# Gate and modulation sums of a hybrid diffusion layer: from per-row multiply-adds with a matmul at the end, to multiply-and-sum along the row with weights laid out by channel

## The chip, the cores and the metric

The kernel runs on one core of one Trainium2 chip. The metric is the device time of one execution in microseconds (us), as a median of runs. The core has a matmul engine (TensorE, PE, whose weight loads are listed as PEld), a vector engine (VectorE, DVE), a scalar engine (ScalarE, ACT), GpSimd (POOL) and SyncE (SP), which here only issues DMAs. ACT issues some DMAs as well.

## The reference

Two layers run over 256 latent tokens and 256 context tokens of width 2048, all in float32. Layer 0 mixes neighbourhood attention (16 heads of 128) with a bidirectional state-space scan (SSD); layer 1 is a gated short convolution. Each layer is modulated by a conditioning vector `c`:

```python
def adaln(cond, w, b):
    m = jax.nn.silu(cond) @ w + b
    return jnp.split(m, 3, axis=-1)          # shift, scale, gate
...
shift, scale, gate = adaln(c, ada_w[i], ada_b[i])
h = modulate(rms_norm(x, norm_g[i]), shift[:, None], scale[:, None])
...
x = x + gate[:, None] * y
```

`ada_w` is 2 x 2048 x 6144. Shift and scale of layer 0 are needed at once, and another part of the kernel makes them. This document is about the rest, which is needed later: the gate of layer 0 (2048 channels), then shift and scale of layer 1 (4096) and its gate (2048). That is one vector of 2048 numbers, silu(c), against 8192 columns of 2048 weights, 64 MB of loads.

## The kernel before, in words

Each float32 weight matrix is loaded in pieces of 128 x 1024 into one of five `raw` buffers (nine at the start), and split into a high part (ACT, L419) and a low part (DVE, L426), so that three fast matmuls make one exact product. PE streams through these pieces: layer 0's input projection for keys, values and queries in eight segments (`ada_gen`, L702, makes the modulated activations for each), then gates, SSD inputs and the remaining heads, then the output projection, layer 1's input projection and its output projection. Attention heads, SSD groups and norms run between, as generators.

Nothing sets the order at run time. While the program is built, a planner (`Plan`, L38) keeps an estimated clock for every engine and for DMA. Work stands in three lists, `urgent`, `side` and `back`; `pump` (L277) writes out a generator's next instructions once the planner thinks that their inputs are ready in time, and each engine then runs its own instructions in the order in which they were written. Names: `W_("DVE", tiles)` means that DVE is about to use these tiles, `when(f)` waits for a condition, `issue` (L364) takes the next load from `loads` (weights) or `later` (the gate and modulation weights) as soon as a buffer is free, `give_raw` returns a buffer, and `hold` keeps the `back` list still at the start and in the norm of layer 1.

The sums of this document are `gemv_gen` (L799), the only task in `back`. `later_loads` (L504) lists its 128 loads, each 256 rows by 512 columns of `ada_w`: the 2048 inputs lie along partitions, the channels along the row. Per load two instructions (L817) multiply one 128 x 512 half with a per-partition scalar (silu(c), in `csil`) and add it to an accumulator `acc`. After 16 loads, two accumulators of 512 channels hold 128 partial sums each. Sixteen matmuls with a matrix of ones (L825) add up the partitions, DVE copies the result (L827), and ACT's DMA (L830) writes it to `mrow` in DRAM. The bias enters as a row loaded into the accumulator (L808). Eight such rounds make 16 blocks of 512 channels. After block 11, shift and scale of layer 1 are read back from DRAM as 32 rows (L835), turned by one PE transpose (L838) and stored in `M1`, one channel per partition. `n_back` tells the readers how far the sums are: `res_gen` (L1587) reads the first gate, `turn_gen` (L1625) `M1`, `fin_gen` (L1957) the second gate.

Of the kernel before, what the change touches and what calls it, by code (L numbers as in the profile page):

```python
# [11 lines left out]
ALU = mybir.AluOpType  # L12
AX = mybir.AxisListType

D = 2048
KB = 16
# [122 lines left out]


@with_exitstack
def kernel(ctx: ExitStack, tc, x, cx, ada0, w0, ada_w, ada_b, w_in, w_out, sc_in, sc_out, rpb, small, const,
                       strict, rows, out):
    nc = tc.nc
    PS = bass.MemoryType.PSUM
# [4 lines left out]
    V, S, G, T, DMA = nc.vector, nc.scalar, nc.gpsimd, nc.tensor, nc.sync  # L150
    DMA2 = nc.scalar
    plan = Plan()
    E = plan.add

    def st(shape, tag, dt=F32, name=None):
        return sb.tile(list(shape), dt, tag=tag, name=name or tag, bufs=1)

    def drt(shape, name):
        return dr.tile(list(shape), F32, name="dram_" + name)


    NTMP, NHALF, NRAW, NW = 9, 8, 5, 3
# [27 lines left out]
    two = lambda ap: ap.rearrange("p (a b) -> p a b", a=2)  # L190
    four = lambda ap: ap.rearrange("p (a b) -> p a b", a=4)

    def mm(o, l, r, start, stop):
        E(T.matmul(o, l, r, start=start, stop=stop, skip_group_check=True))  # L194

    def turn(o, i):
        k = i.shape[0]
        E(T.transpose(o, i, ident if k == 128 else ident[:k, :k]))  # L198
# [136 lines left out]
    def bank():  # L335
        return take(free_b)

    def give(pool, *bs):
        pool.extend(bs)
# [17 lines left out]
    RAW, HL = {}, {}  # L357
# [6 lines left out]
    def issue():  # L364

        while (loads or later) and (free_r or (loads and callable(loads[0]))):
            if loads and callable(loads[0]):
                loads.popleft()()
                continue
            if later and (not loads or (ngem[0] < loads[0][7] and len(RAW) - ngem[0] >= 5 - loads[0][7])):  # L370
                kind, key, w, r0, nb, c0, n = later.popleft()
                ngem[0] += 1
            elif loads:
                kind, key, w, r0, nb, c0, n, _ = loads.popleft()
            else:
                return
            raw = raw_()
            v = raw[:, :nb * n].rearrange("p (b c) -> p b c", b=nb)
            if w is ada0 or w is w0:
# [124 lines left out]
    def later_loads():  # L504
        started[0] = True
        free_r[:] = [a for a in free_r if a.tensor.name not in spare_names]
        for n in range(16):
            lay = 0 if n < 4 else 1
            c0 = 4096 + n * 512 if n < 4 else (n - 4) * 512
            for k in range(8):  # L510
                later.append(("g", ("gem", n, k), ada_w[lay], k * 256, 2, c0, 512))

    CK, CV, CQ, CG = (lambda a: COL_K + a * 512), (lambda a: COL_V + a * 512), (lambda a: a * 512), (lambda a: COL_G + a * 512)

# [276 lines left out]
        got.add(("part", j, key, t))  # L791


    mrow = drt([4, D], "mrow")
    M1 = st([128, 2, KB], "M1")
    accs = st([128, 2, 512], "acc")
    n_back = [0]

    def gemv_gen():  # L799
        for n2 in range(0, 16, 2):  # L800

            yield W_("DVE", nb=0)
            E(V.memset(accs, 0.0))
            for n in (n2, n2 + 1):
                lay = 0 if n < 4 else 1
                c0 = 4096 + n * 512 if n < 4 else (n - 4) * 512
                acc = accs[:, n - n2, :]
                E(DMA.dma_start(acc[:1, :], ada_b[lay:lay + 1, c0:c0 + 512]))  # L808
                for k in range(8):
                    yield when(lambda: not (("gem", n, k) not in RAW))  # L810
                    yield W_("DVE", RAW["gem", n, k][1], acc)
                    raw, v = RAW.pop(("gem", n, k))
                    ngem[0] -= 1
                    for j in range(2):
                        if j:
                            yield W_("DVE", acc)
                        E(V.scalar_tensor_tensor(out=acc, in0=v[:, j], scalar=csil[:, 2 * k + j:2 * k + j + 1], in1=acc,  # L817
                                                 op0=ALU.mult, op1=ALU.add))
# [7 lines left out]
            yield W_("DVE", ps)  # L826
            E(V.tensor_copy(rowb, ps[:, :256]))  # L827
            give(free_b, ps)
            yield W_("AQ", rowb)
            E(DMA2.dma_start(mrow[n // 4, (n2 % 4) * 512:(n2 % 4) * 512 + 1024].rearrange("(m g c) -> g m c", m=2, g=4),  # L830
                             two(rowb[0:128:32, :])))
            n_back[0] = n
            if n == 11:
                yield W_("AQ", mrow[2:3, 1024:])
                E(DMA2.dma_start(mrb[:32, :], mrow[1:3, :].rearrange("r (b c) -> (r b) c", c=128)))  # L835
                yield W_("PE", mrb, nb=1)
                pm = bank()
                turn(pm[:, :32], mrb[:32, :])  # L838
                yield W_("DVE", pm)
                E(V.tensor_copy(M1.rearrange("p r b -> p (r b)"), pm[:, :32]))  # L840
                give(free_b, pm)
                n_back[0] = 11.5

    rowb = st([128, 256], "rowb")
    mrb = rowb[:, :128]

    spawn(back, gemv_gen())
    hold[0] = True
# [1108 lines left out]
    def fin_gen(n, ps):  # L1957
        cols = slice(n * 512, (n + 1) * 512)
        yield when(lambda: n_back[0] >= 15)
        gb, o = tmp(), tmp()  # L1960
        yield W_("SP", mrow[3:4])
        E(DMA.dma_start(gb, mrow[3, cols].partition_broadcast(128)))
# [32 lines left out]
    force(lambda: not urgent, (urgent,))  # L1995


_INS = ['x', 'cx', 'ada0', 'w0', 'ada_w', 'ada_b', 'w_in', 'w_out', 'sc_in', 'sc_out', 'rpb', 'small', 'const', 'strict', 'rows']


# [55 lines left out]
```

## Time and profile before

| | |
|---|---|
| Median of 3 runs | 1769.88 us (1769.78 to 1770.18) |
| Profiled execution | 1768.15 us |
| Its span (first to last instruction) | 1766.2 us |
| PE, DVE, ACT busy in the span | 99%, 71%, 44% |
| The old sums on DVE (L817) | 256 instructions, 191.6 us |
| Their loads | 128 of 512 KB, median 4.3 us from issue to landing |
| First and last sum begin | 166.8 us, 1491.3 us |

A line of instructions reads: line of the kernel, engine, operation, output tile <- input tiles, shapes and count; then busy time and the mean of one in ns, and after the bar the idle time of the engine just before them and what ended it. A timeline line reads: start, length (merged neighbours together), engine, line, operation, and in brackets idle time before it with what ended it. A line of waits reads: who <- whom, then us in total, times, longest. A line of stretches reads: from:to, length, then busy time and count of PE, PEld, DVE, ACT and POOL, then the granted PE clock (1.00 is full), DMA share and GB/s. A line of one source or tile reads: shortest, median and longest duration in ns, first and last start in us. Matmul durations overlap, since the engine is pipelined; the distance between starts tells the rate.

### The profile page before, as it was taken

What the parts mean: (1) busy time and instruction counts of PE and PEld (TensorE: products, weight loads), DVE (VectorE), ACT (ScalarE), POOL (GpSimd) and SP (SyncE); (2) the same over time, 40 slices, a digit from 0 to 9 for tenths busy, and PEclk for the clock granted to TensorE, in tenths of its full rate; (3) what the DMA queues carried; (4) which work ended last, traced back from release to release, by engine and by line L of the source; (5) the groups of instructions that cost most, each with busy time, mean ns of one, the idle gap of its engine ahead of it and who ended that gap; (6) DMA issues with size and microseconds to landing.
All of it is one profiled execution on the core that took longest, in us unless ns stands there. A gap on an engine that the chain in (4) does not pass through costs nothing.

```text
span 1766.2 us, 25384 instructions
## 1 busy us (share of the span) xinstructions
PE 1742.5 (99%) x9577; PEld 1464.8 (83%) x9577; DVE 1260.7 (71%) x1986; ACT 773.2 (44%) x1330; POOL 32.1 (2%) x28
## 2 busy tenths in 40 slices
PE   6999999999999999999999999999999999999998
PEld 4777988888888889888888898888888888888887
DVE  5657778878686878675878787787668776555554
ACT  5423544455242445342445344565445444444442
POOL 0000100001000001000001000000000000000000
PEclk9999999999999999999999999999999999999999
DMA  9977644666746666646666566667867877666563
GB/s 369 347 283 253 209 148 134 200 207 203 233 141 199 205 199 194 220 134 195 209 189 190 159 189 198 194 207 273 294 212 239 264 260 250 189 187 189 190 210 120
DMA packets 218138, 374.60 MB, mean 212 GB/s; under 512 B 32304, under 2 KB 69008, under 8 KB 218016
## 3 DMA queue, kind: packets, MB, share of 16 engines
q1 hardware_dynamic: 210704, 366.38, 64.1%
q10 hardware_dynamic: 7312, 6.61, 1.1%
q8 instruction: 75, 1.23, 0.3%
q14 instruction: 47, 0.39, 0.1%
HBM read 367.52 MB, written 6.72 MB: 212 GB/s over the span
## 4 chain that ended last, share of the span: by engine, by line
PE 90%; DMA 5%; DVE 4%; issue 1%; SPq 1%; ACT 1%; POOL 0%; DVEq 0%; ACTq 0%
PE bank L194 86%; PE bank L198 3%; DMA raw<-in_ada_w 2%; DVE acc L817 1%; DVE w L426 1%; DMA tmp<-dram_csr 1%; DMA raw<-in_w_in 1%; DMA raw<-in_ada 0%; DVE tmp L1241 0%; DMA raw<-in_sc_in 0%; DMA half<-in_rows 0%; SPq L1045 0%; DMA acc<-in_ada_b 0%; ACT w L419 0%; DVE tmp L981 0%
## 5 line engine op out<-in xcount | busy, mean ns | idle before, releaser
L419 ACT CAST w<-raw 128x1024 fp32r<-128x1024 f32 (+1 forms) x343 | 358.2, 1046 | 536.4 <-PE bank L194 458.9
L426 DVE TENSOR_TENSOR w<-raw,w 128x1024 fp32r<-128x1024 f32 (+1 forms) x343 | 414.8, 1213 | 179.7 <-ACT w L419 178.4
L194 PE MATMUL bank<-hH,w 128*128 128x256 f32 (+1 forms) x2064 | 489.2, 324 | 2.5 <-DVE w L426 2.5
L194 PE MATMUL bank<-w,hH 128*128 128x512 f32 x1280 | 405.8, 395 | 2.6 <-ACT hH L757 2.6
L194 PEld LDWEIGHTS bank<-hH,w 128*128 128x128 f32 x2064 | 345.0, 188 | 36.0 <-DVE w L426 3.5
L194 PE MATMUL bank<-hL,w 128*128 128x256 f32 (+1 forms) x1040 | 334.3, 322 | 0.0
L194 PEld LDWEIGHTS bank<-w,hH 128*128 128x128 f32 x1280 | 236.6, 188 | 54.6 <-issue 4.6
L194 PE MATMUL bank<-w,hL 128*128 128x512 f32 x640 | 249.3, 390 | 0.1
L817 DVE SCALAR_TENSOR_TENSOR acc<-raw,csil,acc 128x512 f32<-128x512 f32 x256 | 191.6, 748 | 74.7 <-DMA raw<-in_ada_w 64.2
L194 PEld LDWEIGHTS bank<-hL,w 128*128 128x128 f32 x1040 | 196.4, 189 | 14.9
L194 PE MATMUL bank<-w,h 128*128 128x512 f32 x768 | 180.1, 391 | 0.0
L194 PEld LDWEIGHTS bank<-w,h 128*128 128x128 f32 x768 | 143.4, 188 | 29.8 <-issue 0.4
L194 PEld LDWEIGHTS bank<-w,hL 128*128 128x128 f32 x640 | 120.1, 188 | 25.4 <-DVE hL L763 0.6
L194 PE MATMUL bank<-w,mix 128*128 128x512 f32 x588 | 138.8, 392 | 0.0
L194 PEld LDWEIGHTS bank<-w,mix 128*128 128x128 f32 x588 | 109.4, 188 | 22.6 <-issue 0.2
L1241 DVE SCALAR_TENSOR_TENSOR tmp<-bank,cwh,tmp 128x508 f32<-128x508 f32 (+1 forms) x96 | 71.1, 744 | 1.8
L194 PE MATMUL bank<-KL,h 128*128 128x512 f32 x264 | 63.9, 389 | 0.0
L194 PEld LDWEIGHTS bank<-KL,h 128*128 128x128 f32 x264 | 49.5, 188 | 10.2
L426 DVE TENSOR_TENSOR wL<-raw,wH 128x1024 fp32r<-128x1024 f32 x31 | 37.9, 1222 | 27.6 <-ACT wH L419 27.5
L194 PE MATMUL bank<-QT,h 128*128 128x512 f32 x168 | 55.9, 391 | 0.0
L194 PE MATMUL bank<-wH,h 128*128 128x512 f32 x168 | 55.6, 390 | 0.0
L426 DVE TENSOR_TENSOR QL<-raw,QT 128x1024 fp32r<-128x1024 f32 x32 | 39.1, 1222 | 23.1 <-ACT QT L419 22.6
(288 smaller groups left out, 1976.8 us busy)
## 6 DMA issues: line engine op xcount, KB each, us to landing
raw<-in_w_in SPq DMA_DIRECT2D x196, 512.0 KB, 4.1
raw<-in_ada_w SPq DMA_DIRECT2D x128, 512.0 KB, 4.3
raw<-in_sc_in SPq DMA_DIRECT2D x128, 512.0 KB, 4.6
raw<-in_w_out SPq DMA_DIRECT2D x64, 512.0 KB, 4.2
raw<-in_ada SPq DMA_DIRECT2D x36, 512.0 KB, 5.4
raw<-in_sc_out SPq DMA_DIRECT2D x32, 512.0 KB, 3.7
PT<-in_ada SPq DMA_DIRECT2D x16, 512.0 KB, 8.6
tmp<-dram_csr SPq DMA_DIRECT2D x32, 256.0 KB, 5.8
```

The costliest lines, as they stand in the source:

```text
L194: E(T.matmul(o, l, r, start=start, stop=stop, skip_group_check=True))
L198: E(T.transpose(o, i, ident if k == 128 else ident[:k, :k]))
L419: E(S.copy(H, v))
L426: E(V.tensor_tensor(out=Lo, in0=v, in1=H.bitcast(F32), op=ALU.subtract))
L817: E(V.scalar_tensor_tensor(out=acc, in0=v[:, j], scalar=csil[:, 2 * k + j:2 * k + j + 1], in1=acc, op0=ALU.mult, op1=ALU.add))
L1241: E(V.scalar_tensor_tensor(out=do, in0=di, scalar=cwh[:, 32 * k + ch:32 * k + ch + 1], in1=do, op0=ALU.mult, op1=ALU.add))
```

## The change

The weights for these sums are laid out anew before the launch: `adaT` holds, for each of the 64 blocks of 128 channels and each half of the 2048 inputs, a piece of 128 channels (partitions) by 1024 inputs (along the row). One instruction per load now multiplies a piece with silu(c) and sums along the row (`tensor_tensor_reduce`), into one column of `gp`. For that, silu(c) must lie along the row on every partition. It is turned once into a row by `rows_out` (a PE transpose, a DVE copy, a DMA of ACT to `crow` in DRAM), and half of it at a time is spread over all 128 partitions into `csb` by a DMA of SP. There are three stretches (16, 32 and 16 blocks: gate of layer 0, shift and scale of layer 1, gate of layer 1); in each, all blocks are summed over the first half of the inputs and then over the second, so `csb` is loaded six times. Each stretch ends with two small additions (halves, and the bias, from columns that the kernel already holds in `small`). Shift and scale are then in place in `M1`; the two gates go through `rows_out` to `mrow`. The rounds of sixteen matmuls, the memset of the accumulator, the bias rows, and the way back from DRAM for `M1` are gone. `csb` takes the bytes of `acc`, and `gp` with `rowt` those of `rowb`, so that all other tiles stay at their addresses.

```diff
-        for n in range(16):
-            lay = 0 if n < 4 else 1
-            c0 = 4096 + n * 512 if n < 4 else (n - 4) * 512
-            for k in range(8):
-                later.append(("g", ("gem", n, k), ada_w[lay], k * 256, 2, c0, 512))
+        for q, blocks in enumerate(GEM):
+            for h in range(2):
+                for m in blocks:
+                    later.append(("g", ("gem", m, h), adaT, 2 * m + h, 1, 0, 1024))
...
+    def rows_out(col, dst):
+
+        yield W_("PE", col, nb=1)
+        ps = bank()
+        turn(ps[:16, :128], col)
+        yield W_("DVE", ps)
+        E(V.tensor_copy(rowt[:16, :], ps[:16, :128]))
+        give(free_b, ps)
+        yield W_("AQ", rowt)
+        E(DMA2.dma_start(dst.rearrange("(b c) -> b c", c=128), rowt[:16, :]))
+
     def gemv_gen():
-        for n2 in range(0, 16, 2):
-
-            yield W_("DVE", nb=0)
-            E(V.memset(accs, 0.0))
-            for n in (n2, n2 + 1):
...
-                E(DMA.dma_start(acc[:1, :], ada_b[lay:lay + 1, c0:c0 + 512]))
-                for k in range(8):
...
-                    for j in range(2):
-                        if j:
-                            yield W_("DVE", acc)
-                        E(V.scalar_tensor_tensor(out=acc, in0=v[:, j], scalar=csil[:, 2 * k + j:2 * k + j + 1], in1=acc,
-                                                 op0=ALU.mult, op1=ALU.add))
...
-            yield W_("PE", accs, nb=1)
-            ps = bank()
-            for m in range(2):
-                for g in range(4):
-                    mm(ps[32 * g:32 * g + 32, m * 128:(m + 1) * 128], ONES[:, :32], accs[:, m, g * 128:(g + 1) * 128], m == 0, True)
...
+        yield from rows_out(csil[:, 0:KB], crow[0])
+        for q, blocks in enumerate(GEM):
+            for h in range(2):
+                yield W_("SP", crow, csb)
+                E(DMA.dma_start(csb, crow[0, h * 1024:(h + 1) * 1024].partition_broadcast(128)))
+                for m in blocks:
+                    yield when(lambda: ("gem", m, h) in RAW)
+                    yield W_("DVE", RAW["gem", m, h][0], csb)
+                    raw, _ = RAW.pop(("gem", m, h))
                     ngem[0] -= 1
+                    E(V.tensor_tensor_reduce(out=raw, in0=raw, in1=csb, scale=1.0, scalar=0.0, op0=ALU.mult, op1=ALU.add,
+                                             accum_out=gp[:, h, m:m + 1]))
                     give_raw(raw)
                     issue()
...
+            if q == 1:
+                a, b = p2(16, 32)
+                o = M1.rearrange("p r b -> p (r b)")
+                E(V.tensor_tensor(out=o, in0=a, in1=b, op=ALU.add))
+                E(V.tensor_tensor(out=o, in0=o, in1=P_("ab1")[:, 0:32], op=ALU.add))
+            else:
+                a, b = p2(0 if q == 0 else 48, 16)
+                E(V.tensor_tensor(out=a, in0=a, in1=b, op=ALU.add))
+                E(V.tensor_tensor(out=a, in0=a, in1=P_("ab0" if q == 0 else "ab1")[:, 32:48], op=ALU.add))
+                yield from rows_out(a, mrow[q // 2])
+            n_back[0] = (3, 11.5, 15)[q]
```

In the changed kernel the lines up to L505 move down by one (the split is L420 and L427, matmuls are L195 and transposes L199); the sum is L823, the broadcast L817.

More of the change, by code (lines that the diff above doesn't have):

```diff
@@ L141, with kernel @@
 @with_exitstack
-def kernel(ctx: ExitStack, tc, x, cx, ada0, w0, ada_w, ada_b, w_in, w_out, sc_in, sc_out, rpb, small, const,
+def kernel(ctx: ExitStack, tc, x, cx, ada0, w0, adaT, w_in, w_out, sc_in, sc_out, rpb, small, const,
                        strict, rows, out):
@@ L159, in drt @@
         return dr.tile(list(shape), F32, name="dram_" + name)
+    GEM = (range(0, 16), range(16, 48), range(48, 64))
     NTMP, NHALF, NRAW, NW = 9, 8, 5, 3
@@ L791, in part_gen @@
         got.add(("part", j, key, t))
[L794 removed]
+    mrow, crow = drt([2, D], "mrow"), drt([1, D], "crow")
     M1 = st([128, 2, KB], "M1")
[L796 removed]
+    csb = st([128, 1024], "csb")
+    gp = st([128, 2, 64], "gp")
+    rowt = st([128, 128], "rowt")
     n_back = [0]
[L799 to L818 removed]
@@ L832, in gemv_gen @@
[L832 to L842, printed above, removed]
@@ L844 @@
-    rowb = st([128, 256], "rowb")
-    mrb = rowb[:, :128]
+            yield W_("DVE", gp)
+            p2 = lambda lo, n: (gp[:, 0, lo:lo + n], gp[:, 1, lo:lo + n])
+            if q == 1:
[8 more added lines that the diff above has]
+                yield from rows_out(a, mrow[q // 2])
@@ L1960, in fin_gen @@
         gb, o = tmp(), tmp()
[L1961 to L1962 removed]
+        yield W_("SP", mrow[1:2])
+        E(DMA.dma_start(gb, mrow[1, cols].partition_broadcast(128)))
         for t in range(2):
@@ L1995 @@
     force(lambda: not urgent, (urgent,))
-_INS = ['x', 'cx', 'ada0', 'w0', 'ada_w', 'ada_b', 'w_in', 'w_out', 'sc_in', 'sc_out', 'rpb', 'small', 'const', 'strict', 'rows']
+_INS = ['x', 'cx', 'ada0', 'w0', 'adaT', 'w_in', 'w_out', 'sc_in', 'sc_out', 'rpb', 'small', 'const', 'strict', 'rows']
 def kernel(**inputs):
```

12 lines of the change are left out of this document (4 added, 8 removed).

## The prediction

> **What bounds the kernel now.** I read the page first (busy shares), then the stage table, then the waits of TensorE (PE), then its timeline.
>
> ```profile
> span 1766.2 us, 25384 instructions
> PE 1742.5 (99%) x9577; PEld 1464.8 (83%) x9577; DVE 1260.7 (71%) x1986; ACT 773.2 (44%) x1330; POOL 32.1 (2%) x28
> ```
> ```profile
> 0.00:44.00 44.00, 29.39 (x234) 19.66 (x235) 25.09 (x75) 26.00 (x58) 2.91 (x10) 1.00 0.95 369
> 44.00:88.00 44.00, 44.00 (x298) 32.85 (x297) 29.27 (x58) 17.72 (x34) 0.00 (x0) 1.00 0.92 347
> 1100.00:1400.00 300.00, 299.71 (x1418) 247.86 (x1417) 222.84 (x340) 155.53 (x246) 3.82 (x4) 1.00 0.70 236
> ```
> ```profile
> PE bank L194 <- DVE w L426: 2.5, 2, 1.8
> PE bank L194 <- DVE tmp L1426: 1.1, 1, 1.1
> PE bank L198 <- DVE sgL L1916: 0.7, 1, 0.7
> PE bank L198 <- POOL r L1670: 0.3, 1, 0.3
> ```
> PE is busy from about 44 us to the end, at the full granted clock (1.00). From 166 us on it waits only 2.5 + 1.1 + 0.7 + 0.3 = 4.6 us, in five waits. Outside the first 44 us there is thus almost no idle time to win. What can go is work that PE itself does, and what can come is a new wait of PE. VectorE (DVE) at 71% matters only where it hands PE a tile too late.
>
> **The removed PE work.** The old gate and modulation sums end in eight rounds of 16 small matmuls (128 in all, four column groups in one PSUM bank).
>
> ```profile
> L194 PE MATMUL bank<-acc,const x128: 272/273/298, 379.2 to 1495.4; 128*32 128x128 f32 x128
> ```
> ```profile
> 377.78 0.61 PE L194 MATMUL bank<-w,hH 128*128 128x512 f32 x2
> ...
> 378.46 0.61 PE L194 MATMUL bank<-w,hH 128*128 128x512 f32 x2
> ...
> 379.23 0.64 PE L194 MATMUL bank<-acc,const 128*32 128x128 f32 x16
> 379.81 0.74 PE L194 MATMUL bank<-w,hH 128*128 128x512 f32 x2
> ...
> 380.62 0.63 PE L194 MATMUL bank<-w,hH 128*128 128x512 f32 x2
> ```
> Starts, not durations, show what a round costs, since durations overlap. A group of three wide matmuls repeats every 0.68 us (377.78, 378.46). Without the round the next groups would begin at 379.14 and 379.82; the second begins at 380.62. The round costs 0.80 us. Eight of them: **-6.4 us**. PE is already streaming before and after, so nothing takes this time back.
>
> The old path also turns 32 rows into columns once (L838):
>
> ```profile
> 1106.71 0.62 PE L194 MATMUL bank<-w,hH 128*128 128x512 f32 x2
> ...
> 1107.48 0.24 PE L198 MATMUL bank<-const,rowb 32*128 32x32 f32 x1
> 1107.65 0.73 PE L194 MATMUL bank<-w,hH 128*128 128x512 f32 x2
> ...
> 1108.45 0.62 PE L194 MATMUL bank<-w,hH 128*128 128x512 f32 x2
> ```
> 1106.71 + 0.68 + 0.68 would be the start at 1108.07; it is 1108.45. **-0.38 us.** The change adds three such turns, of 16 columns (`rows_out`). No row shows one; the nearest is this one, so 0.38 us each, with zero as the lower end (a turn in a pause costs nothing). By the built order the first stands right ahead of PE's first projection matmul, in a pause of 1.23 us (quoted below), so two count: **+0.76 us** (0 to 0.76).
>
> [...]
>
> **VectorE.** Removed and added, with the rows that price them:
>
> ```profile
> L817 DVE SCALAR_TENSOR_TENSOR acc<-raw,csil,acc 128x512 f32<-128x512 f32 x256 | 191.6, 748 | 74.7 <-DMA raw<-in_ada_w 64.2
> L426 DVE TENSOR_TENSOR w<-raw,w 128x1024 fp32r<-128x1024 f32 x338 | 411.4, 1221 | 179.7 <-ACT w L419 178.4
> L803 DVE MEMSET acc<- 128x1024 f32 x8 | 7.3, 912 | 1.3 <-issue 0.8 <-DVE half L1128 0.2 <-DMA raw<-in_w_in 0.2
> ```
> ```profile
> L603 DVE CUSTOM_DVE_ANT_0 tmp<-x x8: 681/684/687, 6.1 to 35.2; 128x512 f32<-128x512 f32 x8
> L603 DVE DVE_READ_ACCUMULATOR2_ANT ssq<- x8: 81/82/83, 6.7 to 35.9; 128x1 f32 x8
> ```
> Out go 191.6 + 7.3 = 199 us. In come 128 multiply-and-sum instructions of 128x1024. This width isn't in the trace for this operation; at 512 it takes 0.684 us. Twice that is the upper end, 1.37 us; a plain two-input 128x1024 at 1.22 us is the lower end, and I take 1.22 plus 0.08 for the accumulator read: 167 us. DVE gets about 30 us freer. **0 us** on the path, since PE waits for DVE only 4.3 us after 166 us. One instruction of 1.30 us now stands where two of 0.75 stood, so a weight split behind it can come up to 0.55 us later; the margin below covers that.
>
> How much lateness of DVE does PE forgive? One place shows it:
>
> ```profile
> 229.50 0.42 DVE L1159 TENSOR_TENSOR half<-bank,half 128x256 f32<-128x256 f32 x1 [0.46 <-ACT half L1157]
> 236.04 0.43 DVE L1161 TENSOR_TENSOR half<-half,half 128x256 f32<-128x256 f32 x1 [6.12 <-DMA half<-in_rows]
> 236.38 3.49 DVE L426 TENSOR_TENSOR w<-raw,w 128x1024 fp32r<-128x1024 f32 x3
> ```
> ```profile
> 235.60 0.28 PE L194 MATMUL bank<-hL,w 128*128 128x256 f32 x1
> 237.66 0.50 PE L194 MATMUL bank<-hH,w 128*128 128x256 f32 x2 [1.78 <-DVE w L426]
> ```
> DVE stood still 6.12 us for a DMA with splits queued behind it, and PE lost about 1.9 us (237.66 - 235.60, less the 0.12 us that one such matmul takes in the stream). The margin there is 6.1 - 1.9 = 4.2 us. It agrees with the next row: 45 waits of at most 4.6 us that cost PE next to nothing.
>
> ```profile
> DVE acc L817 <- DMA raw<-in_ada_w: 64.2, 45, 4.6
> ```
>
> **New waits.** The silu row (`crow`) is spread over 128 partitions into one tile, `csb`, six times, half a row each. Its DMA stands in SP's queue and must wait for the last sum that read the old half; the weight loads behind it wait too. But the load issued just ahead of it refills the buffer of that same sum, so SP stands there anyway and only the issue, about 0.5 us, is new. The first sum of the next half waits for the landing, and all later DVE work (the splits that PE needs) queues behind it. The nearest broadcast is that of `csr`, half as large; the nearest of the size are the 512 KB loads:
>
> ```profile
> L1397 SPq DMA_DIRECT2D tmp<-dram_csr x32: 360/460/1456, 364.0 to 1170.1; - x32
> DMA to landing us min/median/max: 5.2/5.8/6.8
> ...
> DMA to landing us min/median/max: 3.4/4.3/9.1
> ```
> The built order has five switches while sums run. At four of them 14 or more DVE instructions (one to four weight splits among them, the rest mostly products and convolution steps) stand between the old half's last sum and the new half's first; that is longer than the landing or close to it. At the fourth broadcast, the middle of the 32-block stretch, only one split stands there. DVE then waits 0.5 + 5.8 - 1.2 = 5.1 us, 0.9 us over the margin: **+0.9 us** (with 3.4: 0; with 9.1: 8.4 - 4.2 = 4.2 us).
>
> **The start.** One ACT-issued DMA (`crow`) now stands ahead of ACT's work for the first context tile, for which PE waits:
>
> ```profile
> 22.98 0.60 ACT L757 ACTIVATE hH<-xm,S,A 128x256 fp32r<-128x256 f32 x1 [0.55 <-DVE S L738]
> 32.82 0.27 ACT L628 COPY xm<-bank 128x128 f32<-128x128 f32 x1 [0.31 <-PE bank L198]
> ```
> ```profile
> 23.63 0.73 PE L194 MATMUL bank<-w,hH 128*128 128x512 f32 x2 [1.23 <-ACT hH L757]
> 34.14 0.50 PE L194 MATMUL bank<-w,hH 128*128 128x512 f32 x1 [1.36 <-ACT hH L757]
> ```
> ```profile
> L830 ACTq DMA_DIRECT2D dram_mrow<-rowb x8: 532/532/1092, 382.1 to 1498.8; - x8
> ```
> ACT idles 0.31 us there, so 0 to 1.1 us; I take **+0.5 us**, its usual issue time. On DVE a 0.91 us memset leaves the same place and a 16-row copy comes, which costs nothing. The first broadcast, 512 KB, falls into a stage that moves 347 GB/s: 0 to 1.5 us; PE shows no wait for a load there, so **0 us**.
>
> All other loads keep their sizes (128 of 512 KB), now one 4 KB run per partition for two of 2 KB: 0 us. Of the small DMAs, SP loses 16 bias loads and gains the six broadcasts, ACT loses eight row writes and a reload and gains two writes beside `crow`: 0 us, since the longest queue for them, SP's, holds ten fewer. Those who read the sums wait on `n_back`; by the built order the last sum comes earlier among PE's work than before, so no reader is held longer.
>
> **Sum**: -6.4 - 0.38 + 0.76 + 0.9 + 0.5 = **-4.6 us**. The profiled execution took 1768.15 us (span 1766.2 and 1.95 around it), so 1763.5; the median of the runs, 1769.88, lies 1.7 us (0.1%) higher, so **1765.3 us**.
>
> **Rivals.**
> 1. The planner deals the work anew. The built order of PE differs from the old one at some 140 places, mostly shifted matmul groups, and the existing waits came from such chances. Another 4.6 us of them gives 1769.9, no change. For: four of the five waits are on DVE. Against: DVE is less loaded. The other way, all gone: 1760.7.
> 2. The small matmuls were hidden (durations overlap, so 99% busy need not mean full): 1769.9, or 1771.3 with the two costs added (0.9 and 0.5). Against: the starts at 379 us. [...]
> 3. **Slower**: the broadcast wait lasts at every switch. Place: first sum after each of five broadcasts. It decides once DVE waits over 4.2 us with splits behind. At 8.4 us each costs 4.2, five 21 us: 1769.9 - 6.0 + 0.5 + 21 = 1785.4. To be slower by 3.5 us each must cost 1.8, a wait of 6.0. For: all splits share DVE's queue. Against: the instructions that stand in between at four of five.
>
> **Chances.** Sum as worked out 0.52; new waits of the planner's 0.22; waits gone 0.08; hidden 0.05; switches 0.13. A measurement of this kernel tells 0.2% (3.5 us) from no change: faster means under 1766.3, slower over 1773.4. Faster takes the forecast less a little (0.47) and the waits gone: 0.55. Same: 0.05 of the forecast, 0.22, 0.05 and the mild part of the switches, 0.02: 0.34. Slower: 0.11. The range goes from all waits gone, 1760.7, to 1772.8, two switches at the upper price (2 x 4.2) in place of one at 0.9; beyond lies most of rival 3.
>
> **What would show it.** Right: no 128*32 128x128 matmuls after 166 us, PE still 99% busy, PE busy about 6 us less; sums at 1.30 us; one long DVE wait for `csb`, at the fourth broadcast. Wrong: PE waits on split tiles (L427) right after each broadcast, or PE waits past 166 us well over 5 us in sum, or sums of 1.37 us with DVE late at many places.

## The result and the profile after

The changed kernel takes 1764.41 us (median of 11 runs, 1760.31 to 1768.90), the kernel before 1769.60 us in the same series. The ratio is 0.9973 (95% interval 0.9963 to 0.9983), or 4.8 us less (3.0 to 6.5). The forecast was 1765.3 us.

The profile after is of the run of 1760.31 us, the quickest of the 11; that matters below. Its page:

```profile
span 1758.5 us, 25025 instructions
...
PE 1736.7 (99%) x9451; PEld 1463.1 (83%) x9451; DVE 1223.6 (70%) x1978; ACT 773.4 (44%) x1330; POOL 31.6 (2%) x28
```

PE is as full as before, with 5.8 us less of busy time and 126 matmul records fewer: 128 small ones and one turn went, three turns came. (The kernel issues eight small matmuls in a round, not sixteen; each float32 matmul stands as two records in the trace. "Sixteen" here and in the forecast counts records.) DVE has 37.1 us less to do (1260.7 - 1223.6). The new sums, by group (busy us, mean ns; then idle time before them), and the lines on `csb` among what the sums waited for (us, times):

```profile
L823 DVE CUSTOM_DVE_ANT_0 raw<-raw,csb 128x1024 f32<-128x1024 f32 x128 | 155.4, 1219 | 26.2 <-DMA raw<-in_adaT 24.0
```
```profile
  DMA raw<-in_adaT: 24.0, 27
  DMA csb<-dram_crow: 1.9, 1
```

A sum takes 1.22 us, plus 0.08 us to read the accumulator: 1.30, as forecast. DVE waited once for a broadcast. Its timeline shows where:

```profile
739.69 1.23 DVE L823 CUSTOM_DVE_ANT_0 raw<-raw,csb 128x1024 f32<-128x1024 f32 x1 [1.86 <-DMA csb<-dram_crow]
```

That is the fourth broadcast, as forecast, but 1.86 us and not 5.1. What PE waited for past 166 us:

```profile
PE bank L195 <- DVE w L427: 2.0, 3, 0.9
PE bank L199 <- POOL r L1664: 0.3, 1, 0.3
```

In this execution that is 2.3 us, against 4.6 before. The two profiles lie 7.84 us apart (1768.15 - 1760.31), three more than the runs' ratio allows: the second profile of the changed kernel, below, shows what the first one was spared.

### The profile page after: what moved, and what is told of

It is laid out like the page before. It is cut to its first block, busy times and chain, and to the rows that moved or that the text cites. A ratio compares the mean times of both kernels' runs of the same rounds, so it can differ in the third digit from the quotient of the medians.

```text
span 1758.5 us, 25025 instructions
## 1 busy us (share of the span) xinstructions
PE 1736.7 (99%) x9451; PEld 1463.1 (83%) x9451; DVE 1223.6 (70%) x1978; ACT 773.4 (44%) x1330; POOL 31.6 (2%) x28
## 4 chain that ended last, share of the span: by engine, by line
PE 94%; DMA 2%; DVE 2%; issue 1%; ACT 0%; POOL 0%; SPq 0%; ACTq 0%; DVEq 0%; POOLq 0%
PE bank L195 91%; PE bank L199 3%; DMA tmp<-dram_csr 1%; DVE w L427 1%; DMA raw<-in_ada 0%; DMA tmp<-dram_exr 0%; DMA raw<-in_adaT 0%; DVE tmp L1235 0%; ACT w L420 0%; POOL statk L572 0%; DVE mix L1562 0%; SPq L583 0%; DVE raw L823 0%; DVE tmp L603 0%; DVE Vt L1012 0%
## 5 line engine op out<-in xcount | busy, mean ns | idle before, releaser
L420 ACT CAST w<-raw 128x1024 fp32r<-128x1024 f32 x343 | 359.5, 1049 | 530.4 <-PE bank L195 447.7
L427 DVE TENSOR_TENSOR w<-raw,w 128x1024 fp32r<-128x1024 f32 x343 | 416.6, 1217 | 231.4 <-ACT w L420 230.1
L195 PE MATMUL bank<-hH,w 128*128 128x256 f32 (+1 forms) x2064 | 488.0, 324 | 1.2 <-DVE w L427 1.1
L195 PE MATMUL bank<-w,hH 128*128 128x512 f32 x1280 | 407.4, 396 | 2.7 <-ACT hH L757 2.5
L195 PEld LDWEIGHTS bank<-hH,w 128*128 128x128 f32 x2064 | 344.7, 188 | 34.2 <-DVE w L427 2.1
L195 PE MATMUL bank<-hL,w 128*128 128x256 f32 (+1 forms) x1040 | 334.3, 321 | 0.0
L195 PEld LDWEIGHTS bank<-w,hH 128*128 128x128 f32 x1280 | 237.7, 189 | 54.4 <-issue 4.0
L195 PE MATMUL bank<-w,hL 128*128 128x512 f32 x640 | 249.9, 391 | 0.1
L195 PEld LDWEIGHTS bank<-hL,w 128*128 128x128 f32 x1040 | 196.3, 189 | 14.9
L195 PE MATMUL bank<-w,h 128*128 128x512 f32 x768 | 179.7, 390 | 0.0
L823 DVE CUSTOM_DVE_ANT_0 raw<-raw,csb 128x1024 f32<-128x1024 f32 x128 | 155.4, 1219 | 26.2 <-DMA raw<-in_adaT 24.0
L195 PEld LDWEIGHTS bank<-w,h 128*128 128x128 f32 x768 | 143.6, 188 | 29.6
L195 PEld LDWEIGHTS bank<-w,hL 128*128 128x128 f32 x640 | 120.5, 188 | 25.4 <-DVE hL L763 0.6
L195 PE MATMUL bank<-w,mix 128*128 128x512 f32 x588 | 138.3, 391 | 0.9 <-DVE w L427 0.9
L195 PEld LDWEIGHTS bank<-w,mix 128*128 128x128 f32 x588 | 109.5, 188 | 24.0 <-DVE w L427 1.3
L195 PE MATMUL bank<-KL,h 128*128 128x512 f32 x264 | 63.8, 389 | 0.0
L427 DVE TENSOR_TENSOR KL<-raw,KL 128x1024 fp32r<-128x1024 f32 x32 | 39.1, 1223 | 33.1 <-ACT KL L420 33.1
L427 DVE TENSOR_TENSOR wL<-raw,wH 128x1024 fp32r<-128x1024 f32 x31 | 37.9, 1224 | 33.5 <-ACT wH L420 33.4
L427 DVE TENSOR_TENSOR QL<-raw,QT 128x1024 fp32r<-128x1024 f32 x32 | 39.2, 1224 | 29.8 <-ACT QT L420 29.8
L195 PEld LDWEIGHTS bank<-KL,h 128*128 128x128 f32 x264 | 49.5, 188 | 10.2
L195 PE MATMUL bank<-QT,h 128*128 128x512 f32 x168 | 56.2, 391 | 0.0
```

The lines of the kernel that those rows point to most:

```text
L420: E(S.copy(H, v))
L427: E(V.tensor_tensor(out=Lo, in0=v, in1=H.bitcast(F32), op=ALU.subtract))
L823: E(V.tensor_tensor_reduce(out=raw, in0=raw, in1=csb, scale=1.0, scalar=0.0, op0=ALU.mult, op1=ALU.add, accum_out=gp[:, h, m:m + 1]))
```

## The experiments

Each kernel ran beside the kernel before on one chip. Ratios are to that kernel, with 95% intervals; 0.001 is 1.8 us. The median of before moved from series to series (1769.6 to 1771.6 us), so kernels of different series are set side by side by their ratios, which adds their uncertainties. Starting theory: the gain is PE work that went. Rivals: the small matmuls were hidden; the relief of DVE; the planner's other order.

**1. Each round three times** (`e1_b_rounds3`), in the kernel before, by plain calls past the planner:

```diff
+            for _ in range(2):
+                for m in range(2):
+                    for g in range(4):
+                        T.matmul(ps[32 * g:32 * g + 32, m * 128:(m + 1) * 128], ONES[:, :32], accs[:, m, g * 128:(g + 1) * 128],
+                                 start=m == 0, stop=True, skip_group_check=True)
```

> The kernel before, with each of the eight rounds of 16 small matmuls written out three times; the planner isn't told, so that the order of all else is as it was. Theory (the rounds are PE work in a full stream, 0.80 us each by the starts): the two further rounds cost 0.63 to 0.80 us each, since only the first pays for the change of the column size; 16 of them, +10.1 to +12.8 us against the kernel before, about 1781, and no new pause of PE. Rival 'hidden' (small matmuls lie beside weight loads): no change, 1769.6. Rival 'relief' (the change gained because DVE has 37 us less to do) and rival 'redeal' (the gain came from the planner's other order) say nothing of a cost here: no change, or less than the theory's.

Measured: 1775.82 us (12 runs), ratio 1.0020 (1.0008 to 1.0031), +3.5 us. Not hidden, but a third of what was expected. PE's timeline at the first round:

```profile
379.63 0.61 PE L194 MATMUL bank<-w,hH 128*128 128x512 f32 x2
...
380.40 0.65 PE L194 MATMUL bank<-acc,const 128*32 128x128 f32 x16
380.87 1.06 PE L829 MATMUL bank<-acc,const 128*32 128x128 f32 x32
381.85 0.74 PE L194 MATMUL bank<-w,hH 128*128 128x512 f32 x2
...
382.67 0.63 PE L194 MATMUL bank<-w,hH 128*128 128x512 f32 x2
```

By the reckoning of the prediction, 382.67 - 379.63 - 2 x 0.68 = 1.68 us for 48 records, against 0.80 for 16. The 32 more cost 0.88 us, eight times 7.0 us, of which the runs show about half; the account of the prediction comes back to this. A record costs 0.027 us there, not 0.05.

**2. Rounds cut to 2 of 8 matmuls, 4 of 16 records** (`e2_b_rounds_short`), the planner told of all eight:

```diff
             for m in range(2):
+                one = T.matmul(ps[0:32, m * 128:(m + 1) * 128], ONES[:, :32], accs[:, m, 0:128], start=m == 0, stop=True,
+                               skip_group_check=True)
                 for g in range(4):
-                    mm(ps[32 * g:32 * g + 32, m * 128:(m + 1) * 128], ONES[:, :32], accs[:, m, g * 128:(g + 1) * 128], m == 0, True)
+                    E(one)
```

> The kernel before with 2 of the 16 matmuls of each round issued; the planner is told of all 16, so the order of all else is as it was. It leaves out the sums over partitions of 14 of 16 groups of channels. Theory: 14 matmuls of 0.80 / 16 = 0.05 us each less, eight times: -5.6 us, or -4.4 us if a part of a round is the change of the column size, which stays; 1764.0 to 1765.2, about as fast as the changed kernel. Hidden: no change, 1769.6. Relief and redeal: DVE's work and the order are those of before, so no change, 1769.6.

Measured: 1770.18 us (12 runs), ratio 0.9996 (0.9981 to 1.0010): no change. By itself this speaks for the rivals, but the timeline of this kernel shows that PE had been spared almost nothing. (The expectation counts 2 of 16; the edit issues 2 of 8, which stand as 4 records.)

```profile
381.13 0.61 PE L194 MATMUL bank<-w,hH 128*128 128x512 f32 x2
...
381.90 0.62 PE L824 MATMUL bank<-acc,const 128*32 128x128 f32 x4
382.46 0.74 PE L194 MATMUL bank<-w,hH 128*128 128x512 f32 x2
...
383.27 0.63 PE L194 MATMUL bank<-w,hH 128*128 128x512 f32 x2
```

383.27 - 381.13 - 1.36 = 0.78 us. A round of two matmuls costs PE nearly as much as one of eight (0.78 against 0.80 us): between these sizes the number of matmuls hardly counts. The run couldn't tell the theories apart.

**3. Rounds put back into the changed kernel** (`e3_a_rounds`), behind every sixteenth sum:

```diff
+                    nsum[0] += 1
+                    if nsum[0] % 16 == 0:
+                        ps = min(free_b, key=lambda t: plan.last[t.tensor.name])
+                        for b in range(2):
+                            for g in range(4):
+                                T.matmul(ps[32 * g:32 * g + 32, b * 128:(b + 1) * 128], ONES[:, :32],
+                                         csb[:, b * 512 + g * 128:b * 512 + (g + 1) * 128], start=b == 0, stop=True, skip_group_check=True)
```

> The changed kernel with a round of 16 small matmuls (csb against ones, into the bank that has been free longest) behind every sixteenth sum, eight in all; nothing reads them and the planner isn't told, so the order of all else is that of the changed kernel. Theory: the gain goes, +6.4 us (0.80 each), 1769.5 to 1770.8, ratio to the kernel before about 1.000. Hidden, relief or redeal: it stays at the changed kernel's 1764.4, ratio 0.997.

Measured: 1767.83 us (12 runs), ratio 0.9976 (0.9965 to 0.9988). By the starts each round again costs 0.80 us, but of these 6.4 us only 0.5 to 2.3 show against the changed kernel's ratios (0.9973, and 0.9963 in experiment 6). The theory missed by this measure.

**4. Half of the old sums** (`e4_b_halfsums`): relief of DVE alone, in the order of before.

```diff
                     for j in range(2):
...
-                        E(V.scalar_tensor_tensor(out=acc, in0=v[:, j], scalar=csil[:, 2 * k + j:2 * k + j + 1], in1=acc,
-                                                 op0=ALU.mult, op1=ALU.add))
+                        if j == 0:
+                            one = V.scalar_tensor_tensor(out=acc, in0=v[:, j], scalar=csil[:, 2 * k + j:2 * k + j + 1], in1=acc,
+                                                         op0=ALU.mult, op1=ALU.add)
+                        E(one)
```

> The kernel before with only the first of the two multiply-adds of each load (128 of 0.748 us less on DVE, 96 us); the planner is told of both, so the order of all else is as it was. It leaves out half of the inputs of every sum. Relief: the change took 37 us from DVE and gained 4.8; 96 us would give that and more, 1765 or less. Theory: PE waited for DVE 4.3 us past 166 us, and the longest such wait ends with a DMA of rows, which stays: 0 to -2 us, 1767.6 to 1769.6.

Measured: 1765.10 us (7 runs), ratio 0.9964 (0.9948 to 0.9979), -6.4 us. Relief gains, against the forecast. All waits of PE in this profile:

```profile
PE bank L194 <- DMA raw<-in_ada: 11.0, 1, 11.0
PE bank L194 <- ACT hH L757: 2.6, 2, 1.4
PE bank L198 <- ACT half L724: 1.0, 2, 0.5
PE bank L198 <- ACT x L613: 0.3, 1, 0.3
PE bank L198 <- POOL r L1672: 0.3, 1, 0.3
```

All those for DVE are gone. By the starts of the same matmuls in this profile and in that of before, PE gains 2.07, 1.49, 1.01 and 0.92 us at the places of before's four longest waits for DVE (237.7, 399.6, 842.6 and 1409.5 us), 5.5 us in all. The first of them stood behind DVE's wait of 6.12 us for a DMA of `half`. DVE now waits less for it:

```profile
234.66 0.42 DVE L1163 TENSOR_TENSOR half<-half,half 128x256 f32<-128x256 f32 x1 [3.64 <-DMA half<-in_rows]
```

That is inside the margin of 4.2 us. The DMA went out at 229.97 us and not at 230.44, though all else of this stretch runs some 1.1 us later in this profile; it stands in SP's queue behind loads for which DVE frees the buffers.

So the theory was widened: PE's lost work, and DVE's lateness, and the order. The next four runs measure the parts.

**5. No rounds at all** (`e5_b_norounds`), in the order of before; `plan` is advanced by hand in place of the call:

```diff
-                    mm(ps[32 * g:32 * g + 32, m * 128:(m + 1) * 128], ONES[:, :32], accs[:, m, g * 128:(g + 1) * 128], m == 0, True)
+                    ki = plan.keys(ONES[:, :32]) + plan.keys(accs[:, m, g * 128:(g + 1) * 128])
+                    ko = plan.keys(ps[32 * g:32 * g + 32, m * 128:(m + 1) * 128])
+                    s = max([plan.t["PE"]] + [plan.w[k] + 60 for k in ki] + [plan.r[k] + 60 for k in ko])
+                    free = plan.t["PE"] = s + 2 * (128 / 1.2) * 0.27 + 80
...
```

> The kernel before with none of the small matmuls (the round with two of sixteen cost as much by the starts as the full one, 0.778 against 0.798 us, so the short rounds took nothing away); DVE copies what the bank held, so the sums over partitions are left out, and the planner is told of the rounds, so that the order of all else is as it was. Theory (a round is 0.79 us of PE's stream, whatever its length): -6.3 us, ratio 0.9964. Rival (the waits for DVE set the pace, and a round moved out of the way is spent in the next wait): PE comes earlier to waits for DVE that end when they did, and 0 to -2 us is left, ratio 0.999 to 1.000.

Measured: 1766.67 us (12 runs), ratio 0.9971 (0.9959 to 0.9983), -5.1 us (3.0 to 7.3). The rounds were on the path. The profiled run, 1772.91 us, is the slowest of the twelve. By the starts of the same matmuls it still gains about 0.8 us at most places where before has a round, but it loses more at stops of PE for DVE, with the granted clock at 0.50 behind two of them. One of the two (timeline and stretch):

```profile
402.73 0.65 PE L194 MATMUL bank<-tmp,xtm 128*64 128x128 f32 x6 [1.47 <-DVE tmp L1436]
```
```profile
404.10:407.50 3.40, 3.40 (x9) 2.53 (x8) 3.08 (x7) 0.63 (x2) 0.69 (x1) 0.50 0.48 152
```

**6. The changed kernel again** (`e6_a_again`), unaltered.

> The changed kernel as it is, on the chip of the other runs of this call, so that those built on it can be set beside it. Ratio to the kernel before 0.9973 as first measured (0.9963 to 0.9983); its profile shows whether the first profile of it, at 1760.31 the fastest of 11 runs, had fewer waits of PE than usual.

Measured: 1764.60 us (10 runs, 1760.12 to 1771.82), ratio 0.9963 (0.9949 to 0.9976). Its profile is of a run of 1765.56 us, 5.3 us longer than the first; by the starts of the same matmuls in both, 4.9 of these come at one place. PE's timeline there, then the stretches (from:to, length, busy time of PE, PEld, DVE, ACT, POOL, granted clock):

```profile
1117.69 4.01 PE L195 MATMUL bank<-w,mix 128*128 128x512 f32 x17
1124.29 0.50 PE L195 MATMUL bank<-w,mix 128*128 128x512 f32 x1 [2.58 <-ACT w L420]
1126.28 4.00 PE L195 MATMUL bank<-w,mix 128*128 128x512 f32 x10 [1.50 <-DVE w L427]
```
```profile
1126.00:1128.00 2.00, 1.72 (x4) 1.43 (x5) 2.00 (x5) 1.98 (x7) 0.00 (x0) 0.50 0.90 231
1128.00:1130.00 2.00, 2.00 (x7) 1.53 (x7) 1.77 (x6) 1.43 (x2) 0.00 (x0) 0.65 0.85 304
```

PE stands still twice, and then runs at half clock. The first profile has a stop of 0.91 us at the same place, the kernel before none. The chain of this profile leads back to a row broadcast, `csr` (start, us, what), and SP's timeline shows what it stood behind:

```profile
1105.55 0.03 issue
1105.58 10.31 DMA tmp<-dram_csr
1115.91 0.69 ACT tmp L1400 x2
1116.61 0.95 ACT w L420
```
```profile
1096.89 7.01 SPq L383 DMA_DIRECT2D raw<-in_w_out  x2
1104.67 0.34 SPq L381 DMA_DIRECT2D raw<-in_adaT  x1
1105.10 0.90 SPq L1391 DMA_DIRECT2D tmp<-dram_csr  x2
```

Two loads wait in SP's queue for their buffers, and `csr` behind them. It lands after 10.3 us (8.0 in the first profile), and the split that PE needs waits behind it in ACT's queue.

**7. One small matmul behind every fourth sum** (`e7_a_32rounds`), 32 in all:

```diff
+                    nsum[0] += 1
+                    if nsum[0] % 4 == 0:
+                        ps = min(free_b, key=lambda t: plan.last[t.tensor.name])
+                        T.matmul(ps[0:32, 0:128], ONES[:, :32], csb[:, 0:128], start=True, stop=True, skip_group_check=True)
```

> The changed kernel with one small matmul (128 rows, 32 columns, csb against ones) behind every fourth sum, 32 in all; nothing reads them, the planner isn't told. Theory: each costs what a round cost, 0.78 us, on PE's stream, +25 us against the changed kernel, ratio to before 1.011. Rival (waits for DVE take the place of what PE saves, and so give way to what it does more): well under that, +5 to +15, ratio 1.000 to 1.006.

Measured: 1777.29 us (5 runs), ratio 1.0042 (1.0029 to 1.0055), 14 us above the changed kernel's 0.9963. By the number this is the rival's range (+5 to +15), not the theory's +25, since by the starts one costs 0.54 us and not 0.78, 17.4 us in all. But of these 17.4 us 14 show, so most of the work added to PE does. A part of the rest is a stop less: in this profile the stop at 1122 us is gone, since PE came there 15 us later.

**8. DVE's relief taken back** (`e8_a_dve_refill`), a copy behind each sum:

```diff
+                    V.tensor_copy(raw[:, 0:256], raw[:, 512:768])
                     give_raw(raw)
```

> The changed kernel with a copy of 128x256 on VectorE behind each sum, into the spent half of its buffer; an estimate of 0.2 to 0.4 us each from the rows of 128x256 (0.41 for a product with two scalars), 26 to 51 us in all, about what the change took from DVE (37). The planner isn't told. Rival 'relief' (the gain is DVE's): it goes, +3 to +5 us against the changed kernel, ratio near 1.000. Theory (PE's work): 0 to +2 us, ratio 0.9973 to 0.9985.

Measured: 1768.06 us (12 runs), ratio 0.9984 (0.9973 to 0.9994), 3.7 us above the changed kernel's 0.9963 and 2.0 above its first 0.9973; both intervals overlap with this one. The ratio lies inside what the theory allowed (to 0.9985), the distance to the changed kernel of the same series inside what relief did (+3 to +5), so the time alone doesn't decide. The group of the copies shows that they take back what the change had freed, 37.7 of 37.1 us:

```profile
L825 DVE COPY raw<-raw 128x256 f32<-128x256 f32 x128 | 37.7, 294 | 4.4
```

The trace shows where the relief went. By the starts of the same matmuls its profiled run (1770.76 us) falls 5.2 us behind that of experiment 6. 4.3 of them come between 400 and 420 us, at two stops of PE for DVE, with the clock at 0.50 for 3.4 us behind the first:

```profile
404.48 0.61 PE L195 MATMUL bank<-const,half 128*128 128x1 f32 x4 [1.85 <-DVE half L1450]
416.51 0.50 PE L195 MATMUL bank<-hH,w 128*128 128x256 f32 x2 [1.72 <-DVE w L427]
```

**9. Broadcasts unknown to the planner** (`e9_a_untold`):

```diff
-                    yield W_("DVE", RAW["gem", m, h][0], csb)
+                    yield W_("DVE", RAW["gem", m, h][0])
```

> The changed kernel, except that the planner isn't told that a sum needs the broadcast (csb), so that it puts less in between at the switches; the rest of the order moves with it. Rival 3 (a wait for csb at every switch, 4.2 us of which PE forgives): DVE waits for csb up to 5.1 us at several switches, more than the one wait of 1.9 us, and PE pays what exceeds 4.2 us, +1 to +5 us against the changed kernel. Theory: the load ahead of the first sum of a half is as late as csb, so that the waits stay under the margin; 0 to +1 us, within what another order gives.

Measured: 1761.13 us (6 runs), ratio 0.9949 (0.9933 to 0.9965), below both of the changed kernel's, though the intervals overlap. Four sums now wait for `csb`, 15.5 us together. The longest two:

```profile
491.80 1.22 DVE L823 CUSTOM_DVE_ANT_0 raw<-raw,csb 128x1024 f32<-128x1024 f32 x1 [6.69 <-DMA csb<-dram_crow]
...
744.13 1.23 DVE L823 CUSTOM_DVE_ANT_0 raw<-raw,csb 128x1024 f32<-128x1024 f32 x1 [5.75 <-DMA csb<-dram_crow]
```

PE's timeline has no wait in the 14 us from 486 and from 738 us. At these places PE forgave 6.69 and 5.75 us, more than 4.2. Rival 3 falls, with its price. The theory's reason falls too: the waits did not stay under the margin.

**10. Another deal** (`e10_a_deal`), the same work with another horizon for the sums:

```diff
-    HOR = ((urgent, 4500.0), (side, 2500.0), (back, 1500.0))
+    HOR = ((urgent, 4500.0), (side, 2500.0), (back, 1200.0))
```

> The changed kernel with another horizon for the list that holds the sums (1200 for 1500), so that the planner deals the same work anew. It shows what another order alone is worth. Theory: the work of PE and DVE stays, so the time stays within some 3 us of the changed kernel's, either way, by the waits of PE that its profile shows. If it lies further off, the order counts for as much as the small matmuls, and the gain of the change is half chance.

Measured: 1773.05 us (12 runs), ratio 1.0009 (0.9999 to 1.0019), some 7 us above the changed kernel. So the theory (3 us to either side) missed: an order alone can take the whole gain back, and by the expectation's own terms the gain of the change is half chance. Two waits of PE that the changed kernel doesn't have, or has shorter:

```profile
PE bank L195 <- ACT wH L420: 4.1, 1, 4.1
PE bank L195 <- DVE w L427: 2.9, 2, 2.7
```

At each of the two longest, near 1324 and 1122 us, the clock stood at 0.50 for 6.8 us.

**11. Both parts in the order of before** (`e11_b_both`), experiment 5 with narrower sums:

```diff
+                        plan.cost = lambda *_: (512 * 1.22 + 70, 90)
-                        E(V.scalar_tensor_tensor(out=acc, in0=v[:, j], scalar=csil[:, 2 * k + j:2 * k + j + 1], in1=acc,
-                                                 op0=ALU.mult, op1=ALU.add))
+                        E(V.scalar_tensor_tensor(out=acc[:, :400], in0=v[:, j, :400], scalar=csil[:, 2 * k + j:2 * k + j + 1],
+                                                 in1=acc[:, :400], op0=ALU.mult, op1=ALU.add))
+                        del plan.cost
...
```

> The kernel before without small matmuls (as the run without rounds) and with multiply-adds of 400 columns in place of 512, about 0.15 us less each, 38 us in all, as much as the change takes from DVE; the planner is told the old costs, so that the order is that of before. It leaves out the sums over partitions and a part of the channels. If both parts count and add: the ratio of the run without rounds (0.9971) less some 2 to 3 us more, 0.9953 to 0.9960, at or below the changed kernel's 0.9963; what the changed kernel then lies above this one is the price of its other order and of the new turns. If relief counts nothing at this order: 0.9971.

Measured: 1761.16 us (8 runs), ratio 0.9955 (0.9940 to 0.9970), 2.8 us below experiment 5's 0.9971. The two intervals overlap, but the trace separates the parts. By the starts of the same matmuls in this profile and in that of before, the eight places of the rounds give 0.52 to 0.95 us each, 6.4 in all; three of before's four waits for DVE give 2.07, 1.01 and 0.92 us, and near the fourth, at 399.6 us, 1.09 us is lost: 2.9 net. (DVE's busy time fell by 26.8 us, to 1233.9, not by 38.)

**12. Two `csr` broadcasts issued by ACT** (`e12_a_csr_on_act`), in the changed kernel:

```diff
-    def add(self, b):
+    def add(self, b, e=None):
...
-        e, op = self.NAMES[str(i.engine).split(".")[-1]], i.opcode
+        e, op = e or self.NAMES[str(i.engine).split(".")[-1]], i.opcode
...
-                E(DMA.dma_start(two(rw), bass.AP(tensor=r0.tensor, offset=r0.offset, ap=[[0, 128], [32 * 256, 2], [1, 256]])))
+                E((DMA2 if (g, b) == (6, 1) else DMA).dma_start(two(rw), bass.AP(tensor=r0.tensor, offset=r0.offset, ap=[[0, 128], [32 * 256, 2], [1, 256]])), "SP")
```

> The changed kernel, except that two of the 32 row broadcasts (csr, the second half of SSD group 6) are issued by ACT and not by SP; the planner is told as before, so that the order of all else stays. In the profiles of the changed kernel they stand in SP's queue behind a weight load and a load of the new sums, which wait for their buffers until 1103.2 and 1104.7 us, and PE stops at 1121 (1.1 us in one profile, 4.1 us and then slow matmuls in the other, where they landed 10 us after issue). ACT idles 4.4 us there, so they go out 3 to 5 us earlier. If SP's queue makes that new wait: the stop at 1121 goes, -1 to -5 us against the changed kernel, 1759 to 1763, ratio to before 0.994 to 0.996. If the late landing is only other traffic: the wait stays, ratio as the changed kernel's, 0.9963 to 0.9973.

Measured: 1760.48 us (6 runs, 1759.52 to 1763.38), ratio 0.9944 (0.9926 to 0.9961). The interval lies below the changed kernel's first one (from 0.9963) and overlaps its second (from 0.9949). Of the changed kernel's 21 runs 14 took over 1764 us, of these six none. The two broadcasts now go out at 1100.28 us, not at 1103.6 or 1105.1:

```profile
1100.28 1.02 ACTq L1391 DMA_DIRECT2D tmp<-dram_csr  x2
```
```profile
1122.88 3.51 PE L195 MATMUL bank<-w,mix 128*128 128x512 f32 x14 [1.06 <-DVE w L427]
```

The slower of the two landed 8.0 us after its issue, as in the first profile, but it had gone out earlier. The short stop of the changed kernel's first profile (0.91 us) is still there, and its chain leads now back to a load of the sums that took 8.1 us to land; the long stop, with the slow matmuls behind it, isn't in this profile. By the starts of the same matmuls this profile gains 4.7 us on that of experiment 6 between 1115 and 1140 us and next to nothing anywhere else but 0.5 us near 685 us. This and experiment 9 have the lowest ratios of all kernels that do the whole work.

## Why the prediction was right, and where it wasn't

- **Eight rounds, -6.4 us**: right. All of them gone gave -5.1 (3.0 to 7.3), and 6.4 by the starts in experiment 11. What the forecast didn't see is what a round's price hangs on: by the starts a round costs 0.78 us with 4 records and 0.80 with 16, so between these sizes the price is nearly fixed. It isn't the same everywhere: 2 records cost 0.54 us, 48 cost 1.68 (with 0.80 for 16, that is 0.44 for each 16 more), and a turn of 16 columns 0.13. That a part of it is the change of the column size, as the expectations of experiments 1 and 2 have it, was the author's estimate and was not shown. Rival 2, that the small matmuls are hidden, fails at these rounds: in the kernel before one costs 0.80 us by the starts.
- **Turns, -0.38 and +0.76 us**: the new ones were priced three times too high. After's timeline around one:

```profile
481.31 0.40 PE L195 MATMUL bank<-hH,w 128*128 128x512 f32 x1
481.55 0.27 PE L199 MATMUL bank<-const,gp 128*16 128x128 f32 x1
481.57 0.48 PE L195 MATMUL bank<-hH,w 128*128 128x512 f32 x1
481.89 0.39 PE L195 MATMUL bank<-hL,w 128*128 128x512 f32 x1
482.12 0.63 PE L195 MATMUL bank<-hH,w 128*128 128x512 f32 x2
```

  The group after 481.31 would begin at 481.99 and begins at 482.12: 0.13 us, twice, so +0.26.
- **VectorE, "0 us on the path"**: this step failed. Taking the freed 37 us back costs 2.0 to 3.7 us (experiment 8), and relief at before's order gains 2.8 and, with 96 us, 6.4 (11 and 4; by the starts 2.9 and 5.5, at the places of the old waits). The row of 4.3 us of waits for DVE was read as small; it is about what relief could give, and it should have been a term, -2 to -4.
- **Wait for `csb`, +0.9 us**: 0. The place was right; the wait was 1.86 us, since this broadcast landed in 4.3 us. The margin of 4.2 us, read at one place, isn't general: 6.69 us were forgiven elsewhere.
- **Start, +0.5 us**: 0. PE's pause for ACT's `hH` at the first context tile is what it was (1.36 us in both profiles), and the turn of silu(c) stands in the earlier pause as forecast:

```profile
21.96 0.27 PE L199 MATMUL bank<-const,csil 128*16 128x128 f32 x1
23.35 0.74 PE L195 MATMUL bank<-w,hH 128*128 128x512 f32 x2 [1.11 <-ACT hH L757]
...
35.13 0.50 PE L195 MATMUL bank<-w,hH 128*128 128x512 f32 x1 [1.36 <-ACT hH L757]
```

  From 23.35 to 35.13 are 11.8 us, against 10.5 before (23.63 to 34.14): in this execution the clock stood at half from 24.6 to 28.0 us. The change isn't the reason, since the second profile of the same kernel takes 10.5 us there, and experiments 4 and 11, built on the kernel before, take 11.8.

- **The planner's redeal**: a rival in the forecast, at 4.6 us to either side. It happened: a new stop near 1122 us, 1 us in one profile and 4.9 with the slow clock behind it in the other, and DVE's old waits gone. Other deals gave about -3 us (not clear of noise) and +7 us against the changed kernel.

With the terms put right the work comes to -6.3 - 0.4 + 0.3 - 3 = -9.4 us for the parts (estimate from the numbers above); measured are -4.8 and -6.6. The first profile, 7.8 us below that of before, would lie 9.1 below it without the 1.3 us lost at its start. The difference of 3 to 5 us to the medians fits what the long stop near 1122 us costs, and experiment 12, without it, is at -9.9 (6.9 to 13.1). So the forecast's -4.6 met the result with the right main term and with two omissions of opposite sign, the relief of DVE and the new stop: that it came so close is in part luck. Its mark of being wrong, "PE waits past 166 us well over 5 us in sum", showed only in the second profile (6.0 us: 3.1 for `w` by L427, 2.6 by L420, and 0.3).

Why did the rounds of experiments 1 and 3 cost less in the medians than by the starts? The mean granted clock of each run answers a part of it. In the profiles each stretch of 3.4 us at half clock lowers it by 0.001: none stands in experiments 1, 3 and 12 (1.000), one in 6 (0.999), two in 5 (0.998), four in 10 (0.996). The table sorts the runs by it.

| Runs at a mean clock of 1.000 | Number | Median, us | Difference, us | By the starts, us |
|---|---|---|---|---|
| Rounds three times (experiment 1) | 5 of 12 | 1775.8 | +6.1 to before (1769.7) | +7.0 |
| No rounds (experiment 5) | 5 of 12 | 1763.7 | -6.1 to before (1769.8) | -6.4 (experiment 11) |
| Rounds put back (experiment 3) | 8 of 12 | 1768.2 | +6.8 to the changed kernel | +6.6 |
| Changed kernel (both series) | 4 of 21 | 1761.4 | | |

So without such stretches the rounds cost about what the starts say. Most runs of the changed kernel have one or more, most of experiment 3 have none, and that hid the rounds in the medians. This sorting was made after the runs, by few of them, and experiment 3 and the changed kernel ran in different series: it supports the theory and doesn't replace a run.

What stays open: by the medians the sizes of the parts are uncertain by some 2 us each. That the stop near 1122 us goes when PE comes later was seen in experiment 7 and, all but 0.59 us of it, in experiment 3, but no run was made for it. What made the broadcasts land late, in 8 to 10 us, was not tried.

## What to carry to other kernels

A few small matmuls of another shape in the middle of a full stream can cost by the break more than by their size (here 0.78 us for two and 0.80 for eight), so count the breaks. An engine's existing waits for another engine can be about what relief of that engine gives (here 4.3 us of waits, and 2.8 and 6.4 us from relief in experiments 11 and 4): put them into the sum. Where a planner deals the work, a gain of 0.3% can be no larger than what another deal gives or takes (here -3 and +7 us): look for the new longest wait, follow it to the queue where a small DMA stands behind a load that waits for a buffer, and move the small one (here a ratio of 0.9944 in experiment 12, against 0.9963 and 0.9973).

## What the runs showed of the hardware

**Behind some short stops PE ran at half clock.** After the stops of experiment 6 the clock stood at 0.50 for 3.4 us (1126.0 to 1129.4 us). Experiment 9 shows the same behind a single stop (timeline and stretch):

```profile
1122.31 3.18 PE L195 MATMUL bank<-w,mix 128*128 128x512 f32 x7 [2.19 <-DVE w L427]
```
```profile
1122.00:1124.00 2.00, 1.69 (x4) 1.30 (x5) 2.00 (x5) 1.73 (x4) 0.00 (x0) 0.64 0.49 156
```

Its next eight wide matmuls start 0.43 us apart and not 0.227, 1.6 us more for a stop of 2.2. The length of the stop alone doesn't decide it: stops of 1.47 us (experiment 5, above) and 1.11 us (at 23.35 us in the first profile of the changed kernel) had such a stretch behind them too. At that second place experiments 2 and 4 show one as well: the mean clock of their first 44 us is 0.96, as in that profile, against 1.00 in the kernel before, which stops there for 1.23 us. A stop of 2.11 us in experiment 1 (at 238.8 us) had none; the mean clock of its whole profile is 1.000. What decides it was not shown.
